# A hybrid attention and convolution layer on one Trainium2 core: x scaled through PSUM, the gate's sigmoid in PSUM, four filter taps a weight chunk, the channel normalisation tied to the last tap

## The chip, the core and the metric

The kernel runs on one core of a Trainium2 chip. The core has a matrix engine (TensorE, PE in the profile, with its weight loads as PEld), three engines for elementwise work (VectorE = DVE, ScalarE = ACT, GpSimd = POOL), and SyncE (SP), whose queue issues most of the loads from memory. On-chip data lies in SBUF or in PSUM; PE writes to PSUM. Each engine runs its own list of instructions in order, and a planner fixes these lists before the kernel runs. The metric is the time of one execution in microseconds; less is better.

## What is computed

One decoder layer over 256 tokens of width 2048, all in float32: a token-mixing part and a squared-ReLU MLP, each between two RMS normalisations. The token-mixing part is this (cut):

```python
a = rms_norm(h, g_mix_pre)
proj = a @ w_in                       # 2048 x 5120
q, k, v, u = ...                      # 1024 + 1024 + 1024 + 2048 columns
attn = moba_attention(q, k, v)        # 8 heads, causal, ALiBi; one block here

val, gt = jnp.split(u + b_glu, 2, axis=-1)
y = val * jax.nn.sigmoid(gt)          # 256 x 1024
y = depthwise_conv(y, w_dw)           # 31 taps, causal
conv = silu(layer_norm(y + b_dw, ln_g, ln_b))

h = h + rms_norm(concat([attn, conv]) @ w_out, g_mix_post)
f = jnp.square(relu(rms_norm(h, g_ffn_pre) @ w_ff1)) @ w_ff2
return h + rms_norm(f, g_ffn_post)
```

## The kernel before

All weights pass through once, as chunks of 128 x 1024 float32 (512 KB). To keep float32 precision, most operands are split into a rounded high part and the low remainder: ACT copies a chunk to its high part `whi` (L123), DVE or POOL subtracts it for the low part `wlo` (L125), and PE multiplies high by high, low by high and high by low. `low_engines` says which engine subtracts; it is a list that the chunks go round. Four buffers hold raw chunks, seven hold split ones; SP loads the next raw chunk when the two parts of an older one have been made. `group_cols` works off a column group of four chunks, `group_rows` one of eight or four chunks with the tokens in rows, `group_words` a group whose weights go into PE unsplit.

Two groups take the first rows of x while they arrive, on x that carries only the gain (`xg`). The factor of each token comes out after all of x: `x_columns` makes it, `token_rows` lays it out as a row on every partition with two PE transposes and copies it to `Rx` (L294). `split_x` then multiplies `xg` by `Rx` in four pieces of 1024 columns (`xn`, L395) and splits each to high and low `xa` (L388, L389). One more group runs unsplit before that (`group_words`, its scaling at L450), and everything from `w_in` behind it needs `xa`.

The gated convolution goes by four groups of 256 channels. `gate_out` takes the sigmoid (L422), `value_out` multiplies value and sigmoid into a padded buffer `hpad` (L427), for group 0 through `glu`, where POOL first scales both by `Rx` (L433). Then `tap_work` puts 62 steps into the list `fillers`: one start on ACT into a PSUM tile `yp` (L405), 60 taps on DVE (L409) and a copy out (L413). `tick` is called after each weight chunk; it first runs what `later(n, ...)` has made due after n chunks, then takes as many steps from `fillers` as `rate` says: five a chunk in the convolution's groups, then three in attention.

Attention follows in two halves of four heads: four column groups for q and k (merged at L254 and L257), scores and softmax (`scores`, L467 to L480), transposes of the weights (`weights_t`, L487), then a row group for v and the products with v (L496, L497). 48 chunks are worked off in it. After the second half `ln_when_ready` looks once a chunk whether `fillers` is empty; when it is, it sends all low parts to DVE, runs `ln_1` (channel mean by a reduction on DVE at L503 and a matmul with ones at L505, subtraction, square) and four chunks later `ln_2` (mean of squares, root, scaling, Silu at L530, split into the upper half of `ma`). Then come three row groups over the attention half of `ma` (`part`, L570), and three over its convolution half (L579), which are the first to read what `ln_2` writes. The rest of the layer is not touched.

Auxiliary PSUM tiles (`aux`) come from one ring of four slots of 128 x 512; `yp`, the transposed row, scores, transposes, products with v and channel means all take one. SBUF tiles with the same `tag` share a ring of `bufs` slots.

The planner keeps to the order of the program where two instructions are ready at once, but moves them on each engine by its own estimate of time.

Of the kernel before, what the change touches and what calls it, by code (L numbers as in the profile page):

```python
# [10 lines left out]
F32 = mybir.dt.float32  # L11
# [4 lines left out]
AX = mybir.AxisListType  # L16

P = 128
S = 256
NT = S // P  # L20
D = 2048
KD = D // P
# [8 lines left out]
G = 512  # L31
# [7 lines left out]
def tile_hybrid_layer(  # L39
# [10 lines left out]
    nc = tc.nc  # L50
# [16 lines left out]
    ph2 = None  # L67

    def aux(name):
        return paux.tile([P, G], F32, tag="aux", name=name)  # L70
# [5 lines left out]
    def acc():  # L76
        return pmain.tile([P, 2, G], F32, tag="mm", name="mm")
# [4 lines left out]
    fillers = deque()  # L82
    rate, credit = [RATE[0]], [0]
    clock = [0]

    def later(n, fn, *args):
        due.setdefault(clock[0] + n, deque()).append((fn, args))

    def tick():
        clock[0] += 1  # L90
        for fn, args in due.pop(clock[0], ()):
            fn(*args)
        credit[0] = min(credit[0] + rate[0], len(fillers))
        while credit[0] >= 1:
            credit[0] -= 1
            fillers.popleft()()


    low_engines = [(nc.vector,)]
# [111 lines left out]
    def mm_words(ps, a, ak, nk, first, last):  # L211

        w = load_raw(nk, 2 * P).rearrange("p (k c) -> p k c", k=nk)
        for j in range(nk):
            for b in range(2):
                nc.tensor.matmul(ps[:, b, :S], w[:, j, b * P:(b + 1) * P], a[:, ak + j, :],  # L216
                                 start=first and j == 0, stop=last and j == nk - 1)
# [33 lines left out]
    def merged(pool, ps, z=None, scale=1.0):  # L251

        tb = pool.tile([P, 2, S], F32, tag="tb", name="tb", bufs=2)
        nc.scalar.activation(tb, ps[:, :, S:], AF.Copy, scale=scale)  # L254
        if z is None:
            z = pool.tile([P, 2, S], F32, tag="z", name="z", bufs=4 if pool is ph2 else 2)
        nc.vector.scalar_tensor_tensor(z, ps[:, :, :S], scale, tb, op0=ALU.mult, op1=ALU.add)  # L257
        return z

    def over(a, n):  # L260
        return a[:, None, :].to_broadcast([P, n, S])
# [27 lines left out]
    def token_rows(rs, dst):  # L289

        p = aux("prow")
        for t in range(NT):
            nc.tensor.transpose(p[:, t * P:(t + 1) * P], rs[t].to_broadcast([P, P]), ident)
        nc.vector.tensor_copy(dst, p[:, :S])  # L294


    cols = const.tile([P, NVEC], F32, name="cols")
# [3 lines left out]
    def col(name, j):  # L301
        return cols[:, VEC_AT[name] + j:VEC_AT[name] + j + 1]
# [16 lines left out]
    xa = apool.tile([P, KD, 2, S], F32R, tag="a", name="xa")  # L319
    p1 = ExitStack()  # L320
    ph1 = p1.enter_context(tc.tile_pool(name="ph1", bufs=1))
    xg = ph1.tile([P, KD, S], F32, tag="ma", name="xg")
# [18 lines left out]
    Rx = const.tile([P, S], F32, name="Rx")  # L341
    r_x = []
# [28 lines left out]

    def first_groups():
        ps = (acc(), acc())
        z = [ph1.tile([P, 2, S], F32, tag="z", name="z", bufs=2) for _ in range(2)]
        k = 0
        for nk in FIRST:
            x_piece(k, nk)
            for g in range(2):
                mm_words(ps[g], xg, k, nk, k == 0, k + nk == KD)
                tick()  # L380
                if k + nk == KD:
                    nc.scalar.activation(z[g], ps[g][:, :, :S], AF.Copy)
            k += nk
        return z

    def split(dst, kb, n, src):
        hi = dst[:, kb:kb + n, 0, :]
        nc.scalar.activation(hi, src, AF.Copy)  # L388
        nc.vector.tensor_sub(dst[:, kb:kb + n, 1, :], src, hi.bitcast(F32))  # L389

    def split_x():
        token_rows(r_x, Rx)
        for k in range(0, KD, 4):
            xn = ph1.tile([P, 4, S], F32, tag="v", name="xn", bufs=2)
            nc.vector.tensor_mul(xn, xg[:, k:k + 4, :], over(Rx, 4))  # L395
            split(xa, k, 4, xn)

    def tap_work(g):

# [17 lines left out]
        fillers.append(done)  # L417

    def gate_out(z, g):
        sig = ph1.tile([P, 2, S], F32, tag="sig", name="sig")  # L420
        for b in range(2):
            nc.scalar.activation(sig[:, b, :], z[:, b, :], AF.Sigmoid, bias=col("bglu", GC + g + b))  # L422
        return sig
# [13 lines left out]
    zg, zv = first_groups()  # L437
# [6 lines left out]
    hpad = yx[:, :GC * (S + PAD)].rearrange("p (g s) -> p g s", g=GC)  # L444
    y = yx[:, GC * (S + PAD):].rearrange("p (g s) -> p g s", g=GC)
    nc.gpsimd.memset(hpad[:, :, :PAD], 0.0)
    later(4, glu, zg, zv, 0)
    ps = group_words(xg)
    z = ph1.tile([P, 2, S], F32, tag="z", name="z", bufs=2)
    nc.vector.tensor_mul(z, ps, over(Rx, 2))  # L450
    low_engines[0], rate[0] = (nc.gpsimd,), RATE[1]
    for i in range(1, 4):
        sig = gate_out(z if i == 1 else merged(ph1, group_cols(xa)), 2 * i)
        value_out(merged(ph1, group_cols(xa)), 2 * i, sig)
    low_engines[0], rate[0] = (nc.vector, nc.gpsimd, nc.gpsimd), RATE[2]


    def head_cols(ps, scale, tag):
# [41 lines left out]

    def channel_mean(src, name):
        tot = lnt(f"tot_{name}")
        nc.vector.reduce_sum(tot, src.rearrange("p g s -> p s g"), axis=AX.X)  # L503
        p = aux(f"pm_{name}")
        nc.tensor.matmul(p[:, :S], ones, tot, start=True, stop=True)  # L505
        return p[:, :S]

    ysq = hpad[:, :, :S]

    def ln_1():  # L510
        mu = lnt("mu")
        nc.vector.tensor_scalar_mul(mu, channel_mean(y, "mu"), 1.0 / CC)
        nc.vector.tensor_sub(y, y, over(mu, GC))
        nc.scalar.activation(ysq, y, AF.Square)
# [19 lines left out]
        for b in range(4):  # L534
            split(ma, GC + 2 * b, 2, ysq[:, 2 * b:2 * b + 2, :])

    def ln_when_ready():
        if fillers:
            later(1, ln_when_ready)
        else:  # L540
            low_engines[0] = (nc.vector,)
            ln_1()
            later(4, ln_2)

    ma = ph1.tile([P, KD, 2, S], F32R, tag="ma", name="ma")
    for half in range(2):
        pTs = []
        for b in range(2):
            qT = head_cols(group_cols(xa), HD ** -0.5, "qT")
            kT = head_cols(group_cols(xa), 1.0, "kT")  # L550
            pT = ph1.tile([P, 2, 3 * P], F32, tag="pT", name="pT", bufs=2)
            pTs.append(pT)
            later(3, scores, 2 * half + b, qT, kT, pT)
        if half:
            later(1, ln_when_ready)
        ps = group_rows(xa, 0, KD)
        v = ph1.tile([P, NT, G], F32, tag="v", name="v", bufs=2)
        nc.scalar.activation(v, ps, AF.Copy)
        later(1, values, half, pTs, v)

    gains = [ph1.tile([P, G], F32, tag=tag, name="gains") for tag in ("qT", "kT", "sig")]
    gains.append(ph1.tile([P, G], F32, tag="z", name="gains", bufs=2))
    for n in range(4):
        nc.gpsimd.dma_start(gains[n], g_mix_post[:, n * G:(n + 1) * G].to_broadcast([P, G]))

    part = []
    for c in range(3):
        ps = group_rows(ma, 0, NH)  # L570
# [130 lines left out]
    for q in range(NQ):  # L701
        ua = ph2.tile([P, KQ, 2, S], F32R, tag="ua", name="ua")
        for c in range(QF // (2 * P)):
# [3 lines left out]
            z = ps_first[c] if c < 2 else merged(ph2, group_cols(ha))  # L707
# [23 lines left out]
FIRST = (1, 1, 2, 2, 2, 2, 2, 2, 2)  # L731


RATE = (2, 5, 3)
AHEAD = 8
HOLD = 6

# [81 lines left out]
```

## Time and profile before

| | |
|---|---|
| Median of three executions | 1079.98 us (1079.85 to 1080.41) |
| Profiled execution: its time | 1080.76 us |
| Profiled execution: span of the core's work | 1079.0 us |
| PE busy | 1054.0 us, 98% of the span |
| DVE busy | 673.8 us, 62% |
| ACT busy | 500.1 us, 46% |
| POOL busy | 244.3 us, 23% |
| Weights and x loaded through SP's queue | 197.3 MB |

A busy share counts an instruction from its start to its modelled end, so a busy PE may still wait inside a matmul. Shares are means over stages with different limits; the views by stage and by line stand below. [...]

### The profile page before, as it was taken

How to read it: one execution, taken by the hardware profiler on the slowest of the kernel's cores; microseconds unless marked ns; L12 is line 12 of the kernel's file. 1: busy time of each engine (PE TensorE's matmuls, PEld its weight loads, DVE VectorE, ACT ScalarE, POOL GpSimd, SP SyncE). 2: the span in 40 equal slices, each digit the busy share in tenths (PEclk: the TensorE clock that was granted, in tenths of full speed). 3: DMA queues.
4: the chain of work that ended last, by engine and by line, in shares of the span. 5: the costliest groups of instructions: out<-in, count | busy, mean ns of one | idle time of the engine just before them, and what ended most of it. 6: DMA issues, size and time to landing. Idle time of an engine off the chain costs nothing.

```text
span 1079.0 us, 14131 instructions
## 1 busy us (share of the span) xinstructions
PE 1054.0 (98%) x5424; PEld 899.0 (83%) x5424; DVE 673.8 (62%) x839; ACT 500.1 (46%) x641; POOL 244.3 (23%) x152
## 2 busy tenths in 40 slices
PE   9999999999899999999999999999999999999996
PEld 8788878888678888888888888888888888888886
DVE  4699993885654886644456555546665445665554
ACT  0454555455654764544444443335443334444440
POOL 6598655551012610100001000001000000100111
PEclk9999999999989999999999999999999999999998
DMA  7655745555464476555666656555656656566642
GB/s 221 200 189 168 258 164 198 171 177 192 156 228 163 155 238 193 181 200 192 194 190 188 190 190 193 194 195 179 196 190 194 195 192 188 186 192 188 195 151 78
DMA packets 58403, 202.41 MB, mean 188 GB/s; under 512 B 6496, under 2 KB 8416, under 8 KB 57952
## 3 DMA queue, kind: packets, MB, share of 16 engines
q1 hardware_dynamic: 57600, 197.32, 56.9%
q0 software_dynamic: 736, 4.19, 1.0%
q8 instruction: 42, 0.69, 0.3%
q14 instruction: 25, 0.20, 0.1%
HBM read 199.39 MB, written 2.10 MB: 187 GB/s over the span
## 4 chain that ended last, share of the span: by engine, by line
PE 89%; DVE 8%; ACT 1%; DMA 1%; issue 0%; DVEq 0%; ACTq 0%
PE mm L190 28%; PE mm L137 14%; PE mm L133 14%; PE mm L136 14%; PE mm L197 14%; DVE yp L409 3%; PE mm L216 3%; DVE wlo L125 1%; DVE xs L600 1%; DMA raw<-in_weights_dram 1%; DVE yx L427 1%; DVE xa L389 0%; PE half L137 0%; PE half L136 0%; PE half L133 0%
## 5 line engine op out<-in xcount | busy, mean ns | idle before, releaser
L125 DVE TENSOR_TENSOR wlo<-raw,whi 128x1024 fp32r<-128x1024 f32 x295 | 376.0, 1276 | 297.3 <-ACT whi L123 297.2
L123 ACT ACTIVATE whi<-raw 128x1024 fp32r<-128x1024 f32 x356 | 375.6, 1058 | 374.0 <-PE mm L137 218.2
L190 PE MATMUL mm<-ha,whi 128*128 128x512 f32 (+1 forms) x1072 | 317.8, 385 | 0.0
L197 PEld LDWEIGHTS mm<-ha,wlo 128*128 128x128 f32 x1024 | 186.4, 188 | 40.4
L197 PE MATMUL mm<-ha,wlo 128*128 128x256 f32 x1024 | 197.0, 279 | 0.0
L136 PE MATMUL mm<-wlo,ua 128*128 128x512 f32 x496 | 193.0, 389 | 0.0
L133 PE MATMUL mm<-whi,ua 128*128 128x512 f32 x496 | 193.0, 389 | 0.0
L137 PE MATMUL mm<-whi,ua 128*128 128x512 f32 x496 | 193.0, 389 | 0.0
L125 POOL TENSOR_TENSOR wlo<-raw,whi 128x1024 fp32r<-128x1024 f32 x61 | 153.8, 2543 | 74.6 <-ACT whi L123 74.2
L649 POOL TENSOR_TENSOR rl<-rl 128x512 f32<-128x512 f32 x32 | 39.4, 1232 | 570.5 <-ACT ua L648 570.5
L190 PEld LDWEIGHTS mm<-ha,whi 128*128 128x128 f32 x1072 | 164.3, 189 | 2.9 <-DVE mg L595 0.2
L190 PE MATMUL mm<-xa,whi 128*128 128x512 f32 x416 | 131.2, 400 | 4.4 <-DVE xa L389 4.4
L133 PEld LDWEIGHTS mm<-whi,ua 128*128 128x128 f32 x496 | 93.1, 188 | 19.3
L136 PEld LDWEIGHTS mm<-wlo,ua 128*128 128x128 f32 x496 | 93.1, 188 | 19.3
L137 PEld LDWEIGHTS mm<-whi,ua 128*128 128x128 f32 x496 | 93.1, 188 | 19.3
L409 DVE SCALAR_TENSOR_TENSOR yp<-yx,cols,yp 128x256 f32<-128x256 f32 x240 | 105.1, 482 | 4.0 <-ACT yp L405 1.5
L197 PEld LDWEIGHTS mm<-xa,wlo 128*128 128x128 f32 x416 | 76.8, 190 | 17.4 <-POOL wlo L125 0.3
L197 PE MATMUL mm<-xa,wlo 128*128 128x256 f32 x416 | 81.2, 281 | 0.0
L190 PEld LDWEIGHTS mm<-xa,whi 128*128 128x128 f32 x416 | 65.2, 190 | 6.0 <-ACT xa L388 2.8
L254 ACT ACTIVATE tb<-mm 128x512 f32<-128x512 f32 x45 | 26.7, 594 | 66.9 <-PE mm L190 66.9
L133 PE MATMUL mm<-whi,ma 128*128 128x512 f32 x128 | 51.4, 404 | 5.5 <-ACT ma L388 5.5
L137 PE MATMUL mm<-whi,ma 128*128 128x512 f32 x128 | 51.0, 400 | 0.1
(166 smaller groups left out, 790.7 us busy)
## 6 DMA issues: line engine op xcount, KB each, us to landing
raw<-in_weights_dram SPq DMA_DIRECT2D x360, 512.0 KB, 4.1
raw<-in_weights_dram SPq DMA_DIRECT2D x14, 256.0 KB, 3.3
xs<-in_x_dram POOLq DMA_DIRECT2D x1, 2048.0 KB, 10.1
xraw<-in_xt_dram SPq DMA_DIRECT2D x7, 256.0 KB, 3.6
gains<-in_g_mix_post_dram POOLq DMA_DIRECT2D x4, 256.0 KB, 4.5
gbc_ffn<-in_g_ffn_post_dram POOLq DMA_DIRECT2D x1, 1024.0 KB, 5.1
out_dram<-fp SPq DMA_DIRECT2D x8, 128.0 KB, 2.0
out_dram<-fp SPq DMA_DIRECT2D x4, 256.0 KB, 2.3
```

What stands on the lines that cost most here:

```text
L123: nc.scalar.activation(hi[:, :n], raw, AF.Copy)
L125: low_engines[0][chunks[0] % len(low_engines[0])].tensor_sub(lo[:, :n], raw, hi[:, :n].bitcast(F32))
L133: m = nc.tensor.matmul(ps, h, wh[:, j, :], start=first and j == 0, stop=False)
L136: nc.tensor.matmul(ps, h, wl[:, j, :], start=False, stop=False)
L137: nc.tensor.matmul(ps, l, wh[:, j, :], start=False, stop=last and j == nk - 1)
L190: m = nc.tensor.matmul(o[:, :, tok], wh[:, j, b * P:(b + 1) * P], a[:, ak + j, :, tok], start=st, stop=en)
L197: nc.tensor.matmul(ps[:, b, :S], wl[:, j, b * P:(b + 1) * P], a[:, ak + j, 0, :], start=False, stop=False)
L216: nc.tensor.matmul(ps[:, b, :S], w[:, j, b * P:(b + 1) * P], a[:, ak + j, :], start=first and j == 0, stop=last and j == nk - 1)
L254: nc.scalar.activation(tb, ps[:, :, S:], AF.Copy, scale=scale)
L409: nc.vector.scalar_tensor_tensor(yp[0][:, b, :], hpad[:, g + b, k:k + S], tap_col(g + b, k), yp[0][:, b, :], op0=ALU.mult, op1=ALU.add)
L427: nc.vector.scalar_tensor_tensor(hpad[:, g + b, PAD:], z[:, b, :], col("bglu", g + b), sig[:, b, :], op0=ALU.add, op1=ALU.mult)
L649: nc.gpsimd.tensor_mul(t, t, t)
```

## The change

The row with the tokens' factors stays in PSUM after the copy, and `split_x` multiplies by it there. The products `xn` are made in eight pieces of 512 columns in PSUM tiles of the auxiliary ring, no longer in four of 1024 in SBUF; the factor row `Rx` in SBUF stays for its other readers. The sigmoid goes to an auxiliary PSUM tile. The SBUF ring for z has three slots for two, and since the sigmoid's SBUF tile is gone, two of the four `gains` tiles lie in it. `glu` of group 0 becomes due five chunks after the first groups and not four.

In attention four steps a chunk are taken from `fillers`, and three of four low parts go to POOL, where it was two of three. The normalisation is no longer polled: `normalise` is the last entry of `fillers`; when it is taken, all low parts go to DVE, `ln_1` is due one chunk later and `ln_2` five. The sum over the eight channel groups is made by three additions of halves, into the buffer `ysq`, and not by one reduction.

```diff
         if z is None:
-            z = pool.tile([P, 2, S], F32, tag="z", name="z", bufs=4 if pool is ph2 else 2)
+            z = pool.tile([P, 2, S], F32, tag="z", name="z", bufs=4 if pool is ph2 else 3)
@@ token_rows
         nc.vector.tensor_copy(dst, p[:, :S])
+        return p[:, :S]
@@
     def split_x():
-        token_rows(r_x, Rx)
-        for k in range(0, KD, 4):
-            xn = ph1.tile([P, 4, S], F32, tag="v", name="xn", bufs=2)
-            nc.vector.tensor_mul(xn, xg[:, k:k + 4, :], over(Rx, 4))
-            split(xa, k, 4, xn)
+        R = token_rows(r_x, Rx)
+        for k in range(0, KD, 2):
+            xn = aux("xn").rearrange("p (k s) -> p k s", k=2)
+            nc.vector.tensor_mul(xn, xg[:, k:k + 2, :], over(R, 2))
+            split(xa, k, 2, xn)
@@
     def gate_out(z, g):
-        sig = ph1.tile([P, 2, S], F32, tag="sig", name="sig")
+        sig = aux("sig").rearrange("p (b s) -> p b s", b=2)
@@
-    later(4, glu, zg, zv, 0)
+    later(GATE_AT, glu, zg, zv, 0)
@@ after the convolution's groups
-    low_engines[0], rate[0] = (nc.vector, nc.gpsimd, nc.gpsimd), RATE[2]
+    low_engines[0], rate[0] = (nc.vector, nc.gpsimd, nc.gpsimd, nc.gpsimd), RATE[2]
@@
     def channel_mean(src, name):
         tot = lnt(f"tot_{name}")
-        nc.vector.reduce_sum(tot, src.rearrange("p g s -> p s g"), axis=AX.X)
+        nc.vector.tensor_add(ysq[:, :4, :], src[:, :4, :], src[:, 4:, :])
+        nc.vector.tensor_add(ysq[:, :2, :], ysq[:, :2, :], ysq[:, 2:4, :])
+        nc.vector.tensor_add(tot, ysq[:, 0, :], ysq[:, 1, :])
@@
-    def ln_when_ready():
-        if fillers:
-            later(1, ln_when_ready)
-        else:
-            low_engines[0] = (nc.vector,)
-            ln_1()
-            later(4, ln_2)
+    def normalise():
+        low_engines[0] = (nc.vector,)
+        later(1, ln_1)
+        later(5, ln_2)
+
+    fillers.append(normalise)
@@ second half of attention
-        if half:
-            later(1, ln_when_ready)
@@
-    gains = [ph1.tile([P, G], F32, tag=tag, name="gains") for tag in ("qT", "kT", "sig")]
-    gains.append(ph1.tile([P, G], F32, tag="z", name="gains", bufs=2))
+    gains = [ph1.tile([P, G], F32, tag=tag, name="gains") for tag in ("qT", "kT")]
+    gains += [ph1.tile([P, G], F32, tag="z", name="gains", bufs=3) for _ in range(2)]
@@
-RATE = (2, 5, 3)
+RATE = (2, 5, 4)
+GATE_AT = 5
```

The tiles z of the first groups and of L449 get three slots in the same way.

## Rows read from the trace of the kernel before

**Rows 1.** Waits of PE, whole span: who waited for whom; total, times, longest (us).

```profile
PE mm L133 <- ACT ma L388: 5.5, 1, 5.5
PE mm L190 <- DVE xa L389: 4.4, 2, 2.6
...
PE ppt L487 <- ACT sc L480: 1.8, 1, 1.8
...
PE psc L467 <- DVE kT L257: 0.6, 1, 0.6
```

**Rows 2.** Chain that ended last, in order of time: start, length (us), what.

```profile
37.22 3.50 DMA raw<-in_weights_dram
...
75.70 0.47 PE mm L197 x4
...
86.86 0.47 PE mm L197 x4
```

**Rows 3.** PE in order of time: start, length (us), line, tile, count, [idle before].

```profile
47.41 0.80 PE L190 MATMUL mm<-xa,whi 128*128 128x512 f32 x2
...
64.63 0.63 PE L197 MATMUL mm<-xa,wlo 128*128 128x256 f32 x4
...
298.37 0.80 PE L133 MATMUL mm<-whi,ma 128*128 128x512 f32 x1 [5.54 <-ACT ma L388]
```

**Rows 4.** Stretches: length, busy PE, PEld, DVE, ACT, POOL; PEclk, DMA share, GB/s.

```profile
58.40:62.20 3.80, 3.80 (x14) 3.18 (x13) 3.76 (x5) 2.81 (x4) 3.80 (x2) 0.57 0.52 176
298.40:304.70 6.30, 6.18 (x14) 4.40 (x15) 4.29 (x6) 3.65 (x6) 0.72 (x1) 0.50 0.49 164
```

**Rows 5.** Stretches of attention, columns as in the group before.

```profile
100.00:156.00 56.00, 53.65 (x308) 46.53 (x307) 55.90 (x115) 28.07 (x40) 35.99 (x16) 1.00 0.56 191
235.00:284.00 49.00, 49.00 (x227) 40.86 (x226) 32.61 (x28) 28.11 (x38) 7.61 (x5) 1.00 0.56 182
```

**Rows 6.** Instructions by line: duration ns min/median/max, first and last start (us), shapes.

```profile
L389 DVE TENSOR_TENSOR xa<-xn,xa x4: 1214/2350/3024, 43.5 to 58.9; 128x1024 fp32r<-128x1024 f32 x4
L389 DVE TENSOR_TENSOR ma<-pav,ma x4: 681/682/691, 190.2 to 265.5; 128x512 fp32r<-128x512 f32 x4
L389 DVE TENSOR_TENSOR ma<-yx,ma x4: 682/682/684, 299.0 to 302.5; 128x512 fp32r<-128x512 f32 x4
L427 DVE SCALAR_TENSOR_TENSOR yx<-z,cols,sig x8: 472/1885/3870, 45.7 to 122.1; 128x256 f32<-128x256 f32 x8
L433 POOL TENSOR_TENSOR z<-z,Rx x2: 2247/2281/2315, 40.2 to 42.5; 128x512 f32<-128x512 f32 x2
L649 POOL TENSOR_TENSOR rl<-rl x32: 1035/1228/1562, 393.9 to 985.8; 128x512 f32<-128x512 f32 x32
L450 DVE TENSOR_TENSOR z<-mm,Rx x1: 678/678/678, 57.9 to 57.9; 128x512 f32<-128x512 f32 x1
L503 DVE TENSOR_REDUCE tot_mu<-yx x1: 3914/3914/3914, 234.9 to 234.9; 128x256 f32<-128x2048 f32 x1
L123 ACT ACTIVATE whi<-raw x356: 1037/1060/1072, 40.7 to 1051.0; 128x1024 fp32r<-128x1024 f32 x178
```

**Rows 7.** DVE in order of time, two products of `value_out` for group 0.

```profile
45.70 5.13 DVE L427 SCALAR_TENSOR_TENSOR yx<-z,cols,sig 128x256 f32<-128x256 f32 x2
```

**Rows 8.** POOL in order of time from 60 us on, low parts of weights.

```profile
56.85 40.22 POOL L125 TENSOR_TENSOR wlo<-raw,whi 128x1024 fp32r<-128x1024 f32 x16
```

**Rows 9.** One stretch for taps alone (DVE) and low parts alone (DVE, POOL).

```profile
100.00:156.00 56.00, 38.52 (x95) 1.00 0.56 191
100.00:156.00 56.00, 13.58 (x7) 34.73 (x14) 1.00 0.56 191
```

**Rows 10.** The two matmuls of the channel means, as by line.

```profile
L505 PE MATMUL pm_mu<-tot_mu,ones x2: 379/380/382, 264.5 to 264.7; 128*128 128x256 f32 x2
L505 PE MATMUL pm_var<-tot_var,ones x2: 377/377/377, 277.7 to 277.9; 128*128 128x256 f32 x2
```

**Rows 11.** ACT in order of time, a load of a function table.

```profile
280.37 1.28 ACT L521 ACT_TABLE_LOAD   x1
```

## Prediction of the change's effect on the time

> **What bounds the kernel now.** I read the waits of the tensor engine (PE) first, because it is busy for 98% of the span. After the start four of them matter [rows 1]: 5.5 us for the first conv block of `ma`, 4.4 us in two waits for `xa`, 1.8 us for a softmax tile, 0.6 us for `kT`. Everything else is weight chunks that follow each other without a gap, so only what removes a wait of PE, or the slow clock after one, can move the end.
>
> Next, what a wait costs in all. Three stages hold them.
>
> *Split stage.* In the steady stretch the marks of two neighbouring column groups stand at 75.70 and 86.86 us, 11.16 us apart [rows 2], which is 2.79 us for each of the group's four chunks. The mark is the group's last run of low products; 0.93 us of the group (two more highs and the next group's first two, as in the chain) lie behind it. The first split group starts at 47.41, so its mark was due at 47.41 + 11.16 - 0.93 = 57.64; it comes at 64.63 [rows 3]. The loss is 7.0 us, or 6.9 if I count back from 75.70. [...]
>
> *First attention pair.* 1.8 + 0.6 = 2.4 us, while the vector engine (DVE) is busy for 55.9 of 56 us [rows 5].
>
> [...]
>
> Sum: 6.9 + 2.4 + 8.6 = **17.9 us**. The change can't give more than that by these stages; the rest of the kernel it doesn't touch.
>
> **Part 1: x scaled and split by way of PSUM.** Why was `xa` late? GpSimd (POOL) works at the same time. Of four identical subtractions the shortest took 1.21 us and the longest 3.02 us; of eight `value_out` products (z and sig both in SBUF) the shortest took 0.47 us, the median 1.89, the longest 3.87 [rows 6], and the first two, 5.13 us together, stand in the middle of the split [rows 7]. POOL suffers too: its two products z*Rx took 2.25 to 2.32 us, where a product of the same shape elsewhere has a median of 1.23 [rows 6]. A DVE product with one operand in PSUM, in the same stage with POOL at work, took 0.68 us for 512 columns [rows 6, 8]. So I price every new DVE step at 0.68: eight products xn and eight subtractions, 16 x 0.68 = 10.9 us, beginning where xn begins now, just after 40 us, and ending near 51. The last pieces are first used by the fourth chunk, at 47.4 + 3 x 2.79 = 55.8. That is 4.8 us of cover; `value_out` for group 0 takes 2 x 0.47 of it if its sigmoid is done by then.
>
> [...]
>
> Slots: the row R and the xn tiles now hold slots of the four-slot auxiliary ring, so three pieces at most are in flight. A piece needs product, copy to high, subtraction, some 3 x 0.68 = 2 us; with three in flight that is 0.7 us a piece, under DVE's 1.36. If planning left only one in flight it would be 8 x 2 = 16 us, ending at 56, right at the need. Behind a product that waits for a slot queue only `value_out` and the first taps.
>
> What is late next is POOL's low parts of the weights. It did 16 of them in 40.22 us, 2.51 each, without a pause [rows 8], against PE's 2.79. z*Rx at 1.23 each would end at 42.7 instead of 44.7. The fourth chunk's buffer comes free with the last word product, about 47.8; its load takes 3.5 us [rows 2], high part 1.05 [rows 6], low part 2.51: 54.9 against 55.8. So the margin is about 1 us, and each later chunk gains 0.28. Bounds of what stays: 0 (all covered) to 3 us (z*Rx still slow, +2, and a piece order that lets the copies wait, +1). I take 0.5, nearest to the covered end. **Gain 6.4.**
>
> **Part 2: sigmoid in PSUM, three z buffers, gate one chunk later.** `value_out` now has one SBUF operand: 8 x 0.47 instead of a median of 1.89. That frees 1.42 us each, some 8 to 11 us of DVE, which is the lag with which DVE enters attention. The third z lets the group's z*Rx leave the accumulator without waiting for group 0's z. `GATE_AT = 5` moves `glu` one chunk on; it comes with the first chunk that uses `xa`, ahead of no needed work. The two `gains` loads that move from sig to z still wait on POOL's queue for a `value_out`; needed only when the parts are scaled, after the conv part, so taken at nothing.
>
> **Part 3: four taps a chunk, three of four low parts on POOL.** The planner's count: 62 steps for each of four groups, 100 run in the 20 chunks before attention, 148 and the new last step are left. At four a chunk `normalise` runs at attention chunk 38; at three (146 left) it came after 49. Can DVE carry four? From 100 to 156 us it did 95 taps and 7 low parts [rows 9] in 56/2.79 = 20 chunks: 4.7 taps and 0.35 low parts a chunk, busy throughout and catching up. Per chunk now: 4 x 38.52/95 = 1.62, a quarter low part at 13.58/7 = 0.49, and the remaining (55.90 - 38.52 - 13.58)/20 = 0.19. That is 2.30 of 2.79 us. So DVE no longer lags, and the 2.4 us of waits go; bounds 0 to 2.4 stay, I take 0.6. **Gain 1.8.** POOL goes to three low parts in four chunks, 7.5 of 11.2 us.
>
> **Part 4: normalisation.** Its first matmul stands in PE's order at 264.5, the second at 277.7 [rows 10], though the taps were done and the sum was being taken at 234.9 [rows 6]: it is the place in program order, chunk 50, that holds it. It moves to chunk 39 and the second to 43, so 11 chunks, some 31 us. From the second matmul to the last subtraction now takes until 302.5 + 0.7, 25.5 us. The change puts the second at 277.7 - 31 - 9 (saved before) = 238, the end at 263; the conv part is needed at 292.8 - 9 = 284. That is 20 us of cover, so the wait and its low clock go: **gain 8.6**, with nothing kept. If the cover were gone, all 8.6 come back.
>
> Its cost in the new place: adds of 1024, 512 and 256 columns, about 1.21 + 0.68 + 0.41 us (the last an estimate: the step from 1024 to 512 columns saves 0.53, the next half of it), replace a reduction of 3.9 us [rows 6]. Every low part from chunk 39 on goes to DVE, which then has 2.79 us for 1.2 us. Between 235 and 284 DVE was busy for 32.6 and ACT for 28.1 of 49 us [rows 5], a stage that already held half of this chain. PE takes both mean matmuls in order, and all weight products queue behind them. Before they stood 13.2 us apart and PE waited at neither; now four chunks, 11.2 us and a little attention work, lie between them, while the sum between them is 1.6 us shorter. Short by 0.4 us, with two low parts of 1.21 us queued ahead on DVE, it would cost 2.8; with the slack that the stage before had, 0. I take 0, since neither shows in [rows 1]. The load of `xs`, which waits in POOL's queue for y, comes earlier with it; no wait of PE for it stands in [rows 1].
>
> ACT gets a new risk: Sqrt and Silu now come while softmax still needs Exp. A table load takes 1.28 us [rows 11]; up to two more, 2.6 us, lie under ACT's 43% idle time and the weight buffers' lead. If ACT had no room for them, PE would get 2.6 us later.
>
> **Sum.** 6.4 + 1.8 + 8.6 = 16.8. The profiled execution took 1080.76 us (span 1079.0), 0.78 above the median; 1080.76 - 16.8 = 1064.0, and on the median 1079.98 - 16.8 = **1063.2**.
>
> **The rivals.**
> *A, new waits in attention (0.18):* the 2.4 us come back and PE waits 2.8 us at a mean matmul: 1063.2 + 1.8 + 2.8 = 1067.8. For: a crowded DVE order set by a plan that doesn't know the slow low parts. Against: 2.30 of 2.79 us.
> *B, the split stays late (0.08):* 3 us kept through POOL or the ring: 1063.2 + 2.5 = 1065.7.
> *C, the tail doesn't go (0.06):* the chain starts earlier but the planner leaves its last steps where they were: 1063.2 + 8.6 = 1071.8. Against: 20 us of cover.
> *D, slower (0.08):* DVE becomes the bound for 37 attention chunks, in the queue where low parts stand behind taps. It takes back 16.8 us from 2.79 + 16.8/37 = 3.24 us of DVE a chunk. With every tap at the 0.48 us of its busy time and every low part as dear as the dearest split step (4 x 0.48 + 3.02/4 + 0.19 = 2.87) it costs 37 x 0.08 = 3 us; above that it needs disorder. At 3.4 us a chunk: 1085.8.
>
> **How the numbers follow.** Forecast 0.60. Its own range is 1061.8 (nothing kept) to 1066. To hold 8 in 10 I reach over A and B and most of the way to C: 1061.5 to 1071. A measurement can tell about 0.2% (2.2 us) from no change: faster than that 0.92 (all but D), within it 0.02 and slower 0.06 (D, split by where a DVE chunk ends).
>
> **What would show it.** Right: `value_out` near 0.47 us, xn and xa steps near 0.68, PE's wait for `xa` gone and the first group's mark near 58; no wait of PE for `ma`, no low clock near 290 to 300; the first mean matmul 35 to 45 us earlier. Wrong: PE waits for `wlo` of POOL near 50 to 60 us, for `kT`, the softmax tile or a column sum in attention, or DVE at 100% through all of attention.

## The result and the profile after

The changed kernel takes 1066.5 us (median of four runs, 1065.6 to 1067.6), the kernel before in the same session 1079.9. The ratio is 0.988 (95% interval 0.987 to 0.989): 13.4 us faster, where 16.8 were forecast. The profiled execution took 1066.0 us, with a span of 1064.2 against 1079.0, so 14.8 us between the two profiles. In the lines of the changed kernel most numbers of the attention part and behind are higher by one.

The waits of PE in the changed kernel (who waited for whom; total, times, longest, us). The first and the third line answer to [rows 1]; the second, on the second half of the kernel, stands in every kernel here.

```profile
PE mm L133 <- ACT part L573: 2.3, 1, 2.3
PE pt L609 <- DVE xs L601: 2.3, 3, 0.8
PE ppt L488 <- ACT sc L481: 1.1, 1, 1.1
```

The waits for `xa` (4.4), `ma` (5.5) and `kT` (0.6) are gone, the one for the softmax tile has fallen from 1.8 to 1.1, and one of 2.3 us is new: for a copy of a partial sum, `part`, in the part behind attention. Then the steps of the split and the first mean matmul, by line (answering to [rows 6] and [rows 10]), and PE in time (to [rows 3]).

```profile
L428 DVE SCALAR_TENSOR_TENSOR yx<-z,cols,sig x8: 470/473/481, 55.5 to 108.8; 128x256 f32<-128x256 f32 x8
L396 DVE TENSOR_TENSOR xn<-xg,prow x8: 685/685/690, 39.6 to 47.9; 128x512 f32<-128x512 f32 x8
L390 DVE TENSOR_TENSOR xa<-xn,xa x8: 679/686/691, 41.9 to 51.5; 128x512 fp32r<-128x512 f32 x8
L508 PE MATMUL pm_mu<-tot_mu,ones x2: 379/380/382, 221.5 to 221.8; 128*128 128x256 f32 x2
```

```profile
47.05 0.81 PE L190 MATMUL mm<-xa,whi 128*128 128x512 f32 x2
...
57.45 0.64 PE L197 MATMUL mm<-xa,wlo 128*128 128x256 f32 x4
```

Every product and subtraction takes 0.68 us and the last one starts at 51.5; before they took 1.2 to 3.0 us for twice the columns. The group's mark comes at 57.45; from its start at 47.05 it is due at 47.05 + 11.16 - 0.93 = 57.28. So 0.2 us of the stage's 7.0 are left. The first mean matmul stands at 221.5 instead of 264.5.

Stretches of the changed kernel (length; busy PE, PEld, DVE, ACT, POOL; granted clock as a share of full speed, DMA share, GB/s), answering to [rows 4] and [rows 5]:

```profile
100.00:156.00 56.00, 54.89 (x311) 47.40 (x310) 54.70 (x113) 29.31 (x43) 36.97 (x17) 1.00 0.55 191
225.00:260.00 35.00, 35.00 (x163) 29.23 (x162) 22.54 (x28) 27.01 (x41) 1.09 (x2) 1.00 0.50 162
255.00:300.00 45.00, 42.67 (x190) 35.03 (x190) 23.66 (x23) 26.86 (x35) 0.73 (x1) 1.00 0.66 225
```

The clock is granted in full in all three. PE misses 1.1 us in the first and 2.3 us in the last, and those are the two waits above. The new one is read from ACT in order of time:

```profile
251.55 1.28 ACT L533 ACT_TABLE_LOAD   x1
252.85 4.04 ACT L533 ACTIVATE yx<-yx,cols 128x256 f32<-128x256 f32 x8
256.91 1.28 ACT L536 ACT_TABLE_LOAD   x1
...
273.93 1.06 ACT L123 ACTIVATE whi<-raw 128x1024 fp32r<-128x1024 f32 x1 [6.92 <-DMA raw<-in_weights_dram]
```

From 251.55 to 258.3 ACT loads the Silu table, does the eight Silu and loads the Sqrt table: 6.8 us, nearly two and a half weight chunks, without a high part. At 273.93 it had stood idle for 6.92 us for the DMA of a raw chunk. Below stand the load of `xs`, which runs at the same time (whether it is a cause is tested among the experiments), the chain's piece for this chunk, and two stretches:

```profile
L577 POOL DMA_DIRECT2D xs<-in_x_dram x1: 726/726/726, 263.9 to 263.9; - x1
```

```profile
264.92 8.91 DMA raw<-in_weights_dram
273.93 1.06 ACT whi L123
274.98 0.92 ACT part L573
```

```profile
266.00:270.00 4.00, 4.00 (x19) 3.34 (x18) 2.89 (x4) 1.01 (x2) 0.00 (x0) 1.00 0.96 379
270.00:274.00 4.00, 3.62 (x16) 2.65 (x15) 0.00 (x0) 0.07 (x1) 0.00 (x0) 1.00 1.01 419
```

The 2 MB of `xs` were issued at 263.9, forty microseconds earlier than before (303.4 there): in both kernels the load waits on POOL's queue for the last subtraction for `ma`, the end of the normalisation (it ends at 263.6 here, 303.2 before). The DMA engines are then full (share 0.96 to 1.01), and the chunk takes 8.91 us where 3.50 stood in [rows 2]. In ACT's list the copy of `part` stands behind the high part of that late chunk: it began at 274.98, where the high part ended, and PE's next matmul at 275.95, behind the copy.

### The profile page after: what moved, and what is told of

Read it like the earlier page. It is cut to its first block, busy times and chain, and to the rows that moved or that the text cites. A ratio compares the mean times of both kernels' runs of the same rounds, so it can differ in the third digit from the quotient of the medians.

```text
span 1064.2 us, 14143 instructions
## 1 busy us (share of the span) xinstructions
PE 1048.5 (99%) x5424; PEld 896.1 (84%) x5424; DVE 662.4 (62%) x855; ACT 500.9 (47%) x646; POOL 227.6 (21%) x148
## 4 chain that ended last, share of the span: by engine, by line
PE 85%; DVE 6%; POOL 3%; ACT 3%; DMA 2%; issue 2%; DVEq 0%; ACTq 0%; POOLq 0%
PE mm L190 25%; PE mm L133 14%; PE mm L137 14%; PE mm L136 14%; PE mm L197 13%; PE mm L216 3%; POOL wlo L125 3%; DVE yp L410 3%; DMA raw<-in_weights_dram 2%; DVE wlo L125 1%; DVE xs L601 1%; ACT whi L123 1%; PE half L137 0%; PE half L136 0%; PE half L133 0%
## 5 line engine op out<-in xcount | busy, mean ns | idle before, releaser
L125 DVE TENSOR_TENSOR wlo<-raw,whi 128x1024 fp32r<-128x1024 f32 x299 | 382.4, 1280 | 288.3 <-ACT whi L123 287.9
L125 POOL TENSOR_TENSOR wlo<-raw,whi 128x1024 fp32r<-128x1024 f32 x57 | 139.2, 2462 | 50.3 <-ACT whi L123 44.7
L133 PE MATMUL mm<-whi,ma 128*128 128x512 f32 x128 | 50.2, 394 | 2.3 <-ACT part L573 2.3
L257 DVE SCALAR_TENSOR_TENSOR z<-mm,tb 128x512 f32<-128x512 f32 x37 | 25.6, 691 | 39.6 <-ACT tb L254 39.6
```

Of the source, the lines that this page charges most:

```text
L125: low_engines[0][chunks[0] % len(low_engines[0])].tensor_sub(lo[:, :n], raw, hi[:, :n].bitcast(F32))
L133: m = nc.tensor.matmul(ps, h, wh[:, j, :], start=first and j == 0, stop=False)
```

## The experiments

Times are medians; "before" is the kernel before, measured beside each group of runs (1079.9 to 1080.1). The first two do one part of the change alone.

**The split by way of PSUM alone.** The kernel before with this edit:

```diff
-        token_rows(r_x, Rx)
-        for k in range(0, KD, 4):
-            xn = ph1.tile([P, 4, S], F32, tag="v", name="xn", bufs=2)
-            nc.vector.tensor_mul(xn, xg[:, k:k + 4, :], over(Rx, 4))
-            split(xa, k, 4, xn)
+        R = token_rows(r_x, Rx)
+        for k in range(0, KD, 2):
+            xn = aux("xn").rearrange("p (k s) -> p k s", k=2)
+            nc.vector.tensor_mul(xn, xg[:, k:k + 2, :], over(R, 2))
+            split(xa, k, 2, xn)
```

> The kernel before with one edit: x is multiplied and split in eight PSUM pieces; sigmoid, taps and normalisation as before. Theory: this edit holds most of the split stage's 6.9 us, so the first group's mark comes at 57.5 to 60 us and PE waits for xa by less than 1 us; 5 to 7 us gained, 1073 to 1075 us. Rival: without the sigmoid in PSUM value_out still takes 5 us of DVE in the middle of the split and the mark stays past 62 us; 2 us gained or less, 1078 to 1080 us.

Measured: 1073.6 us, ratio 0.994 (0.992 to 0.996), 6.4 us faster, with the mark at 57.97. The waits of PE that are left are those of the other two stages:

```profile
PE mm L133 <- ACT ma L389: 5.5, 1, 5.5
...
PE ppt L488 <- ACT sc L481: 2.1, 1, 2.1
```

So this part gives about what was forecast for it, by itself: the four runs lie between 1070.8 and 1075.6 us (the profile is of the slowest), and the interval of the gain is 4.4 to 8.4 us.

**Attention and normalisation alone.** The kernel before with four taps a chunk, three of four low parts on POOL, `normalise` and the halves (the diff ahead of the prediction, without the third z buffer, the split, the sigmoid's tile, `GATE_AT` and the `gains`).

> The kernel before with only the taps and the normalisation changed: four steps a chunk, three of four low parts on POOL, the normalisation as the last step, sums by halves. Theory: the wait for ma (5.5 us and 3.1 us of low clock) goes, the load of xs costs some 2.3 us of it back, the split's 6.9 us stay, and DVE's lag from the split may add up to 2 us of waits in the first attention pair: 1073 to 1076 us. Rival: four taps a chunk need the DVE time that the other edits free; then DVE's lag of 7 us or more reaches PE all through attention, and the time is 1077 us or more, up to slower than before.

Measured: 1076.6 us, ratio 0.997 (0.995 to 0.998): 3.3 us, less than expected. The profile is of its fastest run, 1073.8.

```profile
PE mm L190 <- DVE xa L389: 3.4, 3, 2.6
...
PE mm L133 <- ACT part L571: 2.2, 1, 2.2
PE ppt L487 <- ACT sc L480: 2.1, 1, 2.1
```

The wait for `ma` is gone, but the softmax wait isn't, and the new wait for `part` is there at nearly its full size: it belongs to this part. The two parts alone give 6.4 + 3.3 = 9.7 us, the whole change 13.4. The 3.7 us between them are more than the intervals of the two parts (2.0 and 1.4 us either way) make likely: something in the rest carries them.

**The sigmoid back in SBUF.** The changed kernel with one edit (one of the `gains` tiles goes back into the ring of the sigmoid):

```diff
-        sig = aux("sig").rearrange("p (b s) -> p b s", b=2)
+        sig = ph1.tile([P, 2, S], F32, tag="sig", name="sig")
```

> The changed kernel with the sigmoid back in an SBUF tile (and one gains tile with it). Theory: value_out goes from 0.47 us back to 1.2 to 3.9 us whenever POOL works, which costs DVE about 10 us over the four groups, but the split of x, which has its own products in PSUM, keeps its mark near 57.5 us; DVE enters attention late and the first pair's wait of PE goes from 1.1 us to 2.5 or more: 1067.5 to 1070 us. Rival: the split of the kernel before was late because value_out's 5.1 us stood in its middle, not because of xn and xa; then the first group's mark goes to 61 us or later and the time to 1070 to 1073 us.

Measured: 1077.6 us, ratio 0.998 (0.997 to 0.999). Both readings were far too small: this edit is worth 11 us. The mark of the split stays (57.14); the loss is in attention, shown by PE's waits, the line of `value_out`, and the stretch from 100 to 156:

```profile
PE mm L190 <- DVE qT L257: 3.5, 1, 3.5
PE psc L468 <- DVE sc L471: 3.1, 1, 3.1
```

```profile
L428 DVE SCALAR_TENSOR_TENSOR yx<-z,cols,sig 128x256 f32<-128x256 f32 x8 | 11.6, 1482 | 0.8 <-ACT sig L423 0.7
```

```profile
100.00:156.00 56.00, 48.07 (x254) 40.92 (x253) 56.00 (x112) 21.19 (x24) 34.31 (x16) 0.94 0.51 184
```

The eight products take 11.6 us and not 3.5, DVE is busy for all of 56 us, and PE for 48 of them. With one buffer for two sigmoids the first product came at 62.9 and not at 55.5, so the missing buffer was a rival to the products' price. The next run has two buffers (and two `gains` tiles in that ring):

```diff
-        sig = aux("sig").rearrange("p (b s) -> p b s", b=2)
+        sig = ph1.tile([P, 2, S], F32, tag="sig", name="sig", bufs=2)
```

> The changed kernel with the sigmoid in SBUF in two buffers. The earlier run with one SBUF buffer (1077.6 us) mixed two things: value_out near 1.5 us under POOL, and one buffer for two sigmoids, which made group 0 wait for group 1 (first value_out at 62.9 us, where the changed kernel has 55.5). Theory: the products' price under POOL (8 x about 1 us more) is what matters, so attention still loses about 5 us: 1070 to 1074 us. Rival: the missing buffer was most of it; then 1067 to 1069 us.

Measured: 1076.2 us, ratio 0.996 (0.994 to 0.998). The rival fell, and the theory was too small again: with two buffers the products still take 9.4 us and PE waits 7.1 us in attention. So it is not the number of buffers.

Both runs also show a cost that neither reading had. One low part on DVE takes 7.99 us; here it is in the run with one buffer, with POOL's low parts of the same moment:

```profile
115.64 7.99 DVE L125 TENSOR_TENSOR wlo<-raw,whi 128x1024 fp32r<-128x1024 f32 x1
115.43 7.11 POOL L125 TENSOR_TENSOR wlo<-raw,whi 128x1024 fp32r<-128x1024 f32 x3
```

It begins 0.2 us behind the first of POOL's three and ends 1.1 us behind the last. In the changed kernel no low part on DVE takes more than 3.3 us. POOL's three stand without a pause behind a `gains` load that had waited 1.0 us for `value_out`, since in both runs `gains` tiles lie in the sigmoid's ring; in the changed kernel the two loads of that moment wait for nothing. So what is worth 10 to 11 us is the sigmoid's place together with what it does to POOL's list; the products alone are 5.9 to 8.1 us of DVE, and no run separates the two.

**The split back in SBUF.** The changed kernel with the split's loop of before; the sigmoid stays in PSUM.

```diff
-        R = token_rows(r_x, Rx)
-        for k in range(0, KD, 2):
-            xn = aux("xn").rearrange("p (k s) -> p k s", k=2)
+        token_rows(r_x, Rx)
+        for k in range(0, KD, 4):
+            xn = ph1.tile([P, 4, S], F32, tag="v", name="xn", bufs=2)
```

> The changed kernel (1066.5 us) with x split by way of four SBUF pieces of 1024 columns again; the sigmoid stays in PSUM and the rest as changed. Theory: beside POOL the products and subtractions take 1.2 to 3.0 us each again, the split ends near 56, the first split group's mark comes at 58.5 to 61.5 and not at 57.5, and the time is 1067.5 to 1070.5. Rival: the split was late before only because two slow value_out products stood in its middle; with those moved and cheap, the pieces in SBUF cost nothing: mark at 57.5, 1066 to 1067.5.

Measured: 1072.7 us, ratio 0.993 (0.992 to 0.995), 6.2 us slower than the changed kernel, with the mark at 62.82. DVE in order of time:

```profile
40.25 3.44 DVE L396 TENSOR_TENSOR xn<-xg,Rx 128x1024 f32<-128x1024 f32 x2
43.61 5.59 DVE L390 TENSOR_TENSOR xa<-xn,xa 128x1024 fp32r<-128x1024 f32 x2
49.12 4.54 DVE L396 TENSOR_TENSOR xn<-xg,Rx 128x1024 f32<-128x1024 f32 x2
...
55.56 2.64 DVE L390 TENSOR_TENSOR xa<-xn,xa 128x1024 fp32r<-128x1024 f32 x1
```

No `value_out` stands in the middle here, and the split still ends at 58.2. So the slow steps are its own, beside POOL. From this kernel's start at 47.53 the mark was due at 57.76; it is 5.1 us late, where it was 7.0 before, so the two products of [rows 7] account for 1.9 us at most. PE waits 0.9 us for `xa` here and 1.7 us for POOL's low parts. The direction was as expected, the size was larger.

**Three taps a chunk.** The changed kernel with the rate and POOL's share of before; `normalise` then comes at chunk 50.

```diff
-    low_engines[0], rate[0] = (nc.vector, nc.gpsimd, nc.gpsimd, nc.gpsimd), RATE[2]
+    low_engines[0], rate[0] = (nc.vector, nc.gpsimd, nc.gpsimd), RATE[2]
-RATE = (2, 5, 4)
+RATE = (2, 5, 3)
```

> The changed kernel with three steps a chunk in attention and two of three low parts on POOL, as before; the normalisation is still the last step, so it comes after 50 attention chunks and not 38. Theory: its place decides, so the mean matmuls go back behind the attention part and PE waits for ma again, 5 us or more with low clock behind it: 1072 to 1075 us. Rival: once DVE has no lag, the chain ends in time from there too; then no wait for ma and 1064 to 1067 us.

Measured: 1070.8 us, ratio 0.992 (0.990 to 0.993). PE's waits, and the stretch behind attention:

```profile
PE mm L133 <- ACT ma L389: 5.1, 1, 5.1
```

```profile
262.00:300.00 38.00, 32.79 (x131) 26.06 (x130) 22.42 (x24) 23.83 (x32) 0.72 (x1) 0.91 0.53 174
```

The wait for `ma` is back, with a granted clock of 0.91 over the stretch. No softmax wait is left at three taps. The rate and POOL's share are therefore needed for the place of the normalisation, and, by this one profile, not for the first attention pair.

**The new wait: the load of `xs`.** A first try put the load behind the sum of the first convolution group in the planner's order alone.

> The changed kernel, but the 2 MB load of the token rows xs is issued only after the first conv group's sum (c = 0), some 30 us later than in the changed kernel, where it starts at 263.9 us. Theory: PE's one new wait in the changed kernel (2.3 us before 275.95, behind a weight chunk that took 8.9 us to land where 3.5 is usual) comes from this load, which the earlier normalisation has moved next to a weight stream that was already behind. Then no PE wait over 0.5 us stands between 255 and 300 us and the time is about 1064.2 us, with less spread than 1065.6 to 1067.6. Rival: ACT's eight Silu steps and two table loads (251.5 to 258.3 us, no high part made) alone use up the lead in weights; then a wait of 2 us or more stays and the time stays near 1066.5 us. A load that is now too late for the mix stage would show as a wait for xs near 330 us.

Measured: 1067.4 us, ratio 0.989 (0.987 to 0.990), the wait for `part` 2.1 us. The load still went out at 264.4, so this says nothing about it; it is a second measurement of the changed kernel. The second try makes the load wait for data: DVE writes one element of that sum into `xs` first.

```diff
-    nc.gpsimd.dma_start(xs, x2.rearrange("(t p) d -> p t d", p=P))
     for c in range(3):
         ...
         nc.vector.tensor_add(pc, ps, pc)
+        if c == 0:
+            nc.vector.tensor_copy(xs[:, 0, :1], pc[:, 0, :1])
+            nc.gpsimd.dma_start(xs, x2.rearrange("(t p) d -> p t d", p=P))
```

> The changed kernel with the load of xs held back for real: a copy of one element of the first conv group's sum into xs stands before the load, so the load cannot start before that sum (some 300 us). In the run before, the load kept its place in POOL's list and still started at 264.4 us, so it told nothing of this. Theory: the 2.3 us wait before the conv part comes from the 2 MB that share the memory path with late weight chunks; it falls under 0.5 us and the time to about 1064 to 1065 us. Rival: ACT's stretch without high parts (251.5 to 258.3 us: Silu and two table loads) alone used up the lead; the wait stays at 2 us and the time at 1066 to 1068 us.

Measured: 1062.6 us (1062.1 to 1063.3), ratio 0.984 (0.983 to 0.986): faster than both kernels. The same two stretches:

```profile
100.00:156.00 56.00, 56.00 (x319) 48.74 (x318) 53.13 (x117) 29.66 (x43) 39.60 (x18) 1.00 0.63 204
255.00:300.00 45.00, 45.00 (x202) 37.35 (x201) 25.67 (x25) 28.17 (x37) 2.34 (x3) 1.00 0.59 190
```

PE waits nowhere in them. In the second stretch that is the edit; in the first the edit changes nothing, and what differs is told below.

**The other half of the cause.** The changed kernel with seven of the eight Silu steps left out (seven eighths of the convolution half of `ma` are not made anew); the load stays where it was.

```diff
-        for g in range(GC):
+        for g in range(1):
             last = nc.scalar.activation(ysq[:, g, :], y[:, g, :], AF.Silu,
```

> The changed kernel with seven of the eight Silu steps left out (their channels keep the squares that lie in the buffer), so ACT has 3.5 us less to do just before the conv part; the load of xs keeps its place. If the wait of 2.3 us comes from ACT's stretch without high parts, it goes under 0.5 us, about 1064 us. If it comes from the load of xs alone, it stays near 2 us, about 1066 us. If both are needed, it goes here and in the run with the held load as well.

Measured: 1064.3 us, ratio 0.985 (0.984 to 0.987). The wait for `part` is gone here too, though `xs` loads at its early place. Taking away either one is enough: with the load held, the weights' lead bears ACT's 6.8 us; with the load at its early place, it bears a stretch of 4.7 us without a high part (one Silu, both table loads and the last softmax scaling are in it). It doesn't bear the 6.8 us and the load within 20 us.

**Halves against one reduction, and the order of ACT.** On the version with the load held, the sum of the channels by one reduction again:

```diff
-        nc.vector.tensor_add(ysq[:, :4, :], src[:, :4, :], src[:, 4:, :])
-        nc.vector.tensor_add(ysq[:, :2, :], ysq[:, :2, :], ysq[:, 2:4, :])
-        nc.vector.tensor_add(tot, ysq[:, 0, :], ysq[:, 1, :])
+        nc.vector.reduce_sum(tot, src.rearrange("p g s -> p s g"), axis=AX.X)
```

> The version with the x load held (1062.6 us), with the channel sums made again by one strided reduction each and not by three additions of halves. Theory: the two sums take 3.9 us and not 2.3, the normalisation's chain ends 3 to 4 us later, and some 20 us of cover take it: 1062 to 1063.5, no PE wait for ma. Rival: PE stands at the second mean matmul, because the sum and two queued low parts no longer fit between the two: 1064 to 1066 with a wait for tot_var.

Measured: 1068.8 us, ratio 0.989 (0.988 to 0.991), 6.2 us slower than with halves; both expectations missed the place. PE in order of time, then ACT:

```profile
256.37 1.53 PE L488 MATMUL ppt<-ident,sc 128*128 128x128 f32 x6 [1.63 <-ACT sc L481]
258.36 1.22 PE L497 MATMUL pav<-pT,v 128*128 128x256 f32 x2 [0.47 <-ACT v L556]
```

```profile
249.16 1.28 ACT L531 ACT_TABLE_LOAD   x1
250.45 4.05 ACT L531 ACTIVATE yx<-yx,cols 128x256 f32<-128x256 f32 x8
254.52 1.28 ACT L534 ACT_TABLE_LOAD   x1
...
255.93 1.47 ACT L481 ACTIVATE sc<-sc,sm 128x128 f32<-128x128 f32 x4
257.31 1.00 ACT L556 ACTIVATE v<-mm 128x1024 f32<-128x1024 f32 x1
```

The sum itself is not late. The planner, whose estimates the reduction shifts, has put the Silu stretch ahead of the last softmax scaling and of the copy of v, and PE waits for both. With halves the same list has the scaling at 247.5 and v at 248.9, ahead of Silu at 250.8. To tell the order from the sum, the next run keeps the reduction and ties Silu behind v:

```diff
+    def swish(v):
+        nc.vector.tensor_copy(ysq[:, :, :1], v[:, 0, :GC].rearrange("p (g s) -> p g s", s=1))
         for g in range(GC):
             last = nc.scalar.activation(ysq[:, g, :], y[:, g, :], AF.Silu,
@@ second half of attention, behind the copy of v
+        if half:
+            swish(v)
```

> The version with the x load held and one strided reduction for each channel sum (1068.8 us), with the eight Silu steps tied behind the copy of v on ACT by one copy of eight elements on DVE, so that ACT takes the last softmax scaling and the copy of v first, as it does with halves. Theory: the reduction cost time only through the order of ACT's list, in which Silu with its two table loads, 6.7 us, came ahead of the softmax scaling that PE waited for; with the order restored its 3.9 and 4.1 us lie under cover: 1062 to 1064.5, no PE wait for the softmax tile or v near 255. Rival: the longer sum itself delays the end of the normalisation or fills DVE: 1066 to 1069, with PE waits for ma or tot_var.

Measured: 1064.1 us (1062.2 to 1064.2), ratio 0.985 (0.983 to 0.987). In the profile, which is of the fastest run, the stretch

```profile
225.00:260.00 35.00, 35.00 (x163) 29.26 (x162) 24.45 (x28) 27.00 (x43) 1.09 (x2) 1.00 0.47 151
```

has no wait. 4.7 of the 6.2 us come back. The order's share is 2.1 us of waits and at most some 1.7 us of clock, an estimate from the run without the tie (7 x 0.24):

```profile
255.00:262.00 7.00, 5.02 (x18) 3.79 (x19) 2.71 (x4) 6.99 (x13) 0.00 (x0) 0.76 0.07 9
```

Up to 1.1 us may be the softmax wait of the first pair, which is in the profile of the one and not of the other. The 1.5 us left against the halves lie within overlapping intervals; whether the longer sum costs any of it stays open.

**The gate after four chunks.** The version with the load held, `GATE_AT = 4`.

> The version with the x load held behind the first conv group's sum (1062.6 us), with the gate of group 0 due after four chunks again and not after five. Theory: GATE_AT only moves two value_out products past one weight chunk, both cheap and under the cover of the split's end, so it is worth nothing: 1062 to 1063.5, PE's mark of the first split group stays near 57.5. Rival: the gate in front of the split's last pieces delays them, 1064 to 1067 with PE waits for xa near 50 to 56.

Measured: 1062.6 us (1062.0 to 1062.7), ratio 0.984 (0.982 to 0.985). The later gate is worth nothing that shows; both intervals are some 1.6 us wide to either side.

**The softmax wait of 1.1 us** comes and goes between kernels whose instructions up to 140 us are nearly the same. What goes with it is the time of DVE's own low parts between 100 and 130 us. First the changed kernel, then the one with the load held (length; busy DVE in low parts; clock, DMA share, GB/s):

```profile
100.00:130.00 30.00, 7.37 (x3) 1.00 0.67 233
```

```profile
100.00:130.00 30.00, 3.89 (x3) 1.00 0.73 237
```

The four profiles with the 1.1 us wait for the softmax tile near 149 us (the changed kernel, the planner's-order try, one Silu, one reduction) have 7.4 to 8.3 us there for three low parts; the three without it (load held, gate at four, Silu tied) have 3.5 to 3.9 for three or four. The first of them begins before 100 in each, and only its part behind 100 is counted. The split back in SBUF fits too: 8.75 us for three, and a wait of 1.5.

A low part on DVE takes 1.22 us where POOL stands idle (at 148.16 in the changed kernel) and up to 3.52 beside it (with the load held). Two starts show a difference in their order, first in the changed kernel, then with the load held:

```profile
109.80 2.42 POOL L125 TENSOR_TENSOR wlo<-raw,whi 128x1024 fp32r<-128x1024 f32 x1 [0.58 <-ACT whi L123]
110.02 3.28 DVE L125 TENSOR_TENSOR wlo<-raw,whi 128x1024 fp32r<-128x1024 f32 x1
```

```profile
110.58 1.22 DVE L125 TENSOR_TENSOR wlo<-raw,whi 128x1024 fp32r<-128x1024 f32 x1
110.65 3.41 POOL L125 TENSOR_TENSOR wlo<-raw,whi 128x1024 fp32r<-128x1024 f32 x1 [0.86 <-ACT whi L123]
```

Where POOL began 0.2 us ahead, DVE's ends 1.1 us behind POOL's; where DVE began 0.07 us ahead, it keeps its 1.22 us and POOL's takes 3.41 and not 2.4. So between these two starts a few tenths of a microsecond in phase go with who takes longer. That the softmax wait follows from it is a coincidence over these profiles, not shown: I made no run that shifts the phase alone.

## Why the prediction was right or wrong

**The bound held.** The three stages were read as 17.9 us. The version with the load held, in which PE waits in none of them, is 17.3 us faster than the kernel before. Of the 17.9, the 8.6 us at the head of the conv part are an estimate: 5.54 us in which PE stood still [rows 3] and half of the 6.3 us at a granted clock of 0.50 behind it [rows 4]. No run shows the 8.6 as one figure; with three taps a chunk 5.1 us of waiting came back, with a granted clock of 0.91 over 38 us. The lower end of the forecast's own range doesn't follow from its sum: with nothing kept it is 1079.98 - 17.9 = 1062.1, not 1061.8. The list of waits left out one of 2.3 us for `xs` in the second half of the kernel; the change doesn't touch it. Rival D's 0.48 us a tap is a tap's length from start to end; its busy time in [rows 9] is 0.41.

**Part 1 was right in size and in reason.** 6.4 us forecast, 6.4 measured alone (4.4 to 8.4), 6.2 when taken out. Steps at 0.68 us, an end near 51 and a mark near 58 came as told, and POOL's margin of 1 us sufficed: no PE wait for POOL's low parts in the split. One detail was off: `value_out` of group 0 came at 55.5, not right behind the split, as it waited 3.3 us for the sigmoid behind ACT's table load (1.28 us at 51.51); it was covered. The subtraction's median is 0.686 us from PSUM, against 0.682 from SBUF in [rows 6], 0.004 us apart. The steps went from 1.2 to 3.0 us for 1024 columns with two inputs in SBUF to a steady 0.68 us for 512 with one, with POOL at work in both.

**Part 2 was right as a duration and priced at the wrong place.** "Frees 8 to 11 us of DVE" was forecast; the eight products took 14.0 us in the kernel before and 3.5 in the changed one, 10.5 us less (taken out of the whole, 8.1 with one buffer and 5.9 with two). But the sum gave this part nothing of its own and put the 1.8 us of attention under the four taps. Taken out of the whole, the sigmoid's place (with the `gains` and the bunched low parts that come with it) costs 10 to 11 us, the largest of all edits. The third z buffer has no run of its own.

The step that failed is in part 3: "So DVE no longer lags". The count of 2.30 us a chunk would make 46 us of the 56 from 100 to 156; in the changed kernel DVE is busy for 54.70 of them and without a pause until 140, with 95 taps done where four a chunk make 80. It enters attention behind and is still catching up, even with the cheap products. With the sigmoid in SBUF it is the slower rival D in small: DVE busy for 56.00 of 56 us.

The same lag is a reason why the parts don't add up. Alone, the split gives 6.4 us at three taps; added to the tail with the sigmoid in SBUF it gave 0.4 (1076.6 against 1076.2). In these two profiles the waits for `xa`, 3.4 us, go, and those in attention grow from 2.9 (2.1 + 0.8) to 7.1 (2.7 + 2.6 + 1.8), which fits a delay of PE's own that had hidden DVE's. The low part of 7.99 us is in the second of the two only, so how much of the growth is the lag alone stays open.

**Part 3** was given 1.8 with 0.6 kept; 1.1 stays in four of seven profiles and nothing in three. At three taps PE waits 2.1 and 0.6 us with the sigmoid in SBUF (the split alone) and not at all with it in PSUM (three taps a chunk). That is one profile each, but it puts the gain with the sigmoid and not with the taps.

**Part 4 was right in its mechanism and mis-sized by what came with it.** The mean matmuls moved by 43 and 40 us (35 to 45 were forecast), the last subtraction for `ma` starts at 262.9 (263 was forecast for its end), and wait and low clock are gone. "With nothing kept" was wrong by 2.3 us. Two sentences carried it. The load of `xs` was seen to come earlier and taken at nothing because no PE wait for it stood in [rows 1]: but the thing to ask was what it collides with at its new place, not what it met at its old one. And the table loads were laid under ACT's idle share and the weights' lead, without counting that the Silu stretch makes them one block of 6.8 us in which no high part is made. One extra table load came (8 in the whole run against 7), not two. Each would have been hidden; together they used up the lead.

The account between the two profiles: 6.8 (split) + 1.3 (softmax wait 1.8 to 1.1, and `kT`'s 0.6) + 6.3 (8.6 less 2.3) = 14.4 of the 14.8 us; PE's earlier start, 47.05 for 47.41, is the rest. Against these 14.4 the forecast's 16.8 has 2.3 us too much in part 4 and 0.5 in attention, and 0.4 too little in the split. The medians differ by 13.4 as the profiled run of the kernel before lies above its median and that of the changed kernel below.

Of the rivals, A had half of its mechanism (the softmax wait) but no wait at a mean matmul; B, C and D didn't come in the changed kernel.

## What to carry to other kernels

When a step is moved, follow every transfer that hangs on it to its new place and ask what that place already lacks: two covers that each suffice can fail together when they draw on the same lead. Price an edit by taking it out of the finished whole, not only by doing it alone; a lag that hides behind another engine's delay can come out as waits as soon as that engine is on time. Before believing that a longer instruction costs its length, compare the order of the other engines' lists, since a planner may have turned two of them round.

## What the runs showed of the hardware

Beside a 2 MB load issued through POOL's queue a 512 KB chunk of weights took 8.91 us, against 3.50 in [rows 2], with the DMA share at 0.96 to 1.01. With the load held back, PE waits nowhere in that stretch. The same subtraction of 1024 columns took DVE 1.22 us when it began 0.07 us ahead of one on POOL, 3.28 us when it began 0.2 us behind one (ending 1.1 us after it), and 7.99 us when it began 0.2 us behind the first of three on POOL without a pause (again ending 1.1 us after the last).
